# One small matmul moved ahead of a product: the MLP norm's mean between the first products of two blocks

## The chip, the cores and the metric

The kernel runs on one core of a Trainium2 chip. The time is the device time of one execution in microseconds (us). One further execution was recorded by the hardware profiler; its time line (the trace) and its summary page are what the profile is here.

## The reference

The kernel computes a small decoder trunk in float32 for 512 tokens of width 1024. Two layers follow one another, the first with a multi-head latent attention mixer (MLA), the second with gated linear attention (GLA); each has a squared-ReLU MLP with 4096 hidden columns:

```python
def rms_norm(x, gain):
    y = xf * lax.rsqrt(jnp.mean(xf * xf, axis=-1, keepdims=True) + EPS)
    return (y * gain).astype(x.dtype)
def sq_relu_mlp(xn, w_up, w_down):
    hid = jnp.square(jax.nn.relu(xn @ w_up))
    return hid @ w_down
...
        x = x + mix.astype(x.dtype)
        x = x + sq_relu_mlp(rms_norm(x, norm_mlp[i]), mlp_w_up[i], mlp_w_down[i]).astype(x.dtype)
    return rms_norm(x, final_norm)
```

## The kernel before

**Layout.** The residual stream is held transposed, as 8 tiles `xT[j]` of 128 features by 512 tokens. A float32 matrix is cut into a rounded part and a remainder (`split`: ScalarE writes the high part, line 112, VectorE the low part, line 115), and a product is taken as high times high, high times low and low times high. In the MLP these matmuls have 256 columns and are issued by line 826 (`matmuls`): 24 for each product, 16 with the high part of the weights (`wh`) and 8 with the low part (`wl`). "Product" below means such a run of 24.

**The MLP.** The up projection goes through blocks of 512 hidden columns, `up_block(b)` for b = 0 to 7. A block is a list of steps s0 to s7, which form its result with seven products in place of eight (a Strassen scheme: the names 11, 21, 22, T1 to T4 are quadrants of the normalised input and their combinations, prepared by class `QuadNorm`). The down projection is split in the same way (`down_block`, whose left operand is the tile `h`, 48 matmuls to a product). `mlp` pops the steps of the blocks from lists in an order written out by hand.

**The norm.** The gain is applied to the operands at once, the root of the mean only where a product is finished (`finish`, lines 887 to 891, which multiplies by `rstd`). `square` sums the squares of the 8 tiles in `acc` (line 238, VectorE); `mean` (line 255) multiplies `acc` by a matrix of 1/1024, which leaves the mean in a PSUM bank; `Norm.finish` and `rsqrt` (lines 211 to 221) turn it into `rstd` with two ScalarE and three VectorE operations. The float32 matmul of the mean appears as two records in the trace.

**Start of the MLP.** The last output projection of the mixer adds into `xT[7]`, and its square is the last that goes into `acc`. Meanwhile two matmuls whose result is not used (line 1163) and the first product of block 0 run (`s1`: operand tiles x0 to x3, weights `wh` and `wl`). The first product of block 1 has its weights in a tile named `w`, which takes the place that the combination T3 gets afterwards (`s0`, line 907). `combine` and `combined` then form T3 on VectorE and ScalarE.

**Order.** A planner orders the instructions of each engine by their place in the program and by its own estimate of when their inputs are there. `keep_in_program_order` (`kept`) pins an instruction behind the one written before it on the same engine; the first matmul of every product is pinned so (line 839), and so is the mean. On TensorE the order around the change is thus fixed by the text.

**Places in memory.** The pools hold a few spacers (`PADS`, `pad`). The tile `h1` is made 40 elements (160 bytes) longer than needed, and `operand` uses it from element 0 for the first product of a down block that takes this tile, and from element 40 for the others:

```python
                h = dp.tile([P, 8 * TH + 40], F32R, tag="h1", name=uname("h"))
                c = 0 if turn[1] != s else 40
```

Of the kernel before, what the change touches and what calls it, by code (L numbers as in the profile page):

```python
# [49 lines left out]
def trunk_kernel(ctx: ExitStack, tc: tile.TileContext, t_in: dict, out: bass.AP, out_row: bass.AP):  # L50
# [22 lines left out]
    def uname(s):  # L73
        count[0] += 1
        return f"{s}_{count[0]}"
# [69 lines left out]
    def piece(raw, a, n, order=lambda i: i):  # L145
        hi = sb.tile([P, a, n], F32R, tag="wh", bufs=3, name=uname("wh"))
        lo = sb.tile([P, a, n], F32R, tag="wl", bufs=3, name=uname("wl"))
        cut_at.append(split(raw, hi, lo, order=order))
        return hi, lo
# [183 lines left out]
    nrm = Norm(ND, inv_d, "mix", 0, "A")  # L333
# [475 lines left out]
    def mlp(layer, nrm, nxt, final=False):  # L809
# [337 lines left out]
        blocks = [up_block(b) for b in range(NB)]  # L1147
# [18 lines left out]
        for b, t in enumerate(halves(wide_raw())):  # L1166
            fills[b](t)
        kept = tc.keep_in_program_order
        for b in range(2):
            blocks[b].pop(0)()  # L1170
        t = nrm.combine(KH - 1, dp.tile([P, 4, TH], F32, tag="q", bufs=6, name=uname("q")))
        kept(nrm.mean())
        made[1]["21"] = piece(made[1]["a12"], KH, 256)
        kept(cut_at[-1])
        kept(nrm.combined(KH - 1, t))
# [466 lines left out]
    n_mix1 = Mixer(ND, inv_d, "mix", ND, "A")  # L1642
    n_mlp0 = mlp_norm(0)
    mlp0 = mlp(0, n_mlp0, n_mix1)
    out_proj(t_in["mla_w_o"][0], O, n_mlp0, mlp0, begun)
    next(mlp0, None)
# [5 lines left out]
    class Final:  # L1652
# [39 lines left out]
        def row(self, t, c, p):  # L1692
# [19 lines left out]
            for eng, q, cs in ((ACT, ACT, slice(0, 384)), (DVE, SP, slice(384, D))):  # L1712
# [4 lines left out]
                q.dma_start(o[:, cs], y[:, cs])  # L1717

    mlp1 = mlp(1, n_mlp1, Final(), True)
    out_proj(t_in["gla_w_o"][0], Y, n_mlp1, mlp1)  # L1720
    next(mlp1, None)
# [53 lines left out]
```

## Time and profile before

| what | value |
|---|---|
| runs | 1065.54, 1066.1, 1068.97 us; median 1066.1 us |
| the profiled execution's own time | 1065.53 us |
| its span, first to last instruction | 1063.8 us |
| TensorE matmul busy (PE) | 1055.4 us, 99% |
| weight loads (PEld) | 975.8 us, 92% |
| VectorE (DVE) | 856.6 us, 81% |
| ScalarE (ACT) | 642.4 us, 60% |
| mean granted TensorE clock | 0.998 |

Rows of the trace's time line give the start in us from the span's start, the duration in us, the engine, the line, the operation, the tile written and the tiles read, the shape, and how many like instructions are merged (x2). Buffer numbers are left out of names; for a matmul, the moving operand stands first and the weights second (`ps<-x0h,w`). PEld rows are weight loads; a load runs ahead of the matmul that uses it. Matmuls overlap in the pipeline, so a row's duration is longer than the distance to the next row's start; the pace of the array is the distance between starts.

### The profile page before, as it was taken

How to read it: one execution, taken by the hardware profiler on the slowest of the kernel's cores; microseconds unless marked ns; L12 is line 12 of the kernel's file. 1: busy time of each engine (PE TensorE's matmuls, PEld its weight loads, DVE VectorE, ACT ScalarE, POOL GpSimd, SP SyncE). 2: the span in 40 equal slices, each digit the busy share in tenths (PEclk: the TensorE clock that was granted, in tenths of full speed). 3: DMA queues.
4: the chain of work that ended last, by engine and by line, in shares of the span. 5: the costliest groups of instructions: out<-in, count | busy, mean ns of one | idle time of the engine just before them, and what ended most of it. 6: DMA issues, size and time to landing. Idle time of an engine off the chain costs nothing.

```text
span 1063.8 us, 17962 instructions
## 1 busy us (share of the span) xinstructions
PE 1055.4 (99%) x7332; PEld 975.8 (92%) x7332; DVE 856.6 (81%) x1186; ACT 642.4 (60%) x937; POOL 78.8 (7%) x104
## 2 busy tenths in 40 slices
PE   9999999999999999999999999999999999999997
PEld 7788988999999999988788888888999999999986
DVE  6789879899799789967565654678999799799965
ACT  6577645575667777644334734655665667776734
POOL 7400001000000000030000000001000000000000
PEclk9999999999999999999999999999999999999999
DMA  7312017765553663360222211238665555654412
GB/s 219 91 50 80 7 34 217 165 193 145 173 141 118 179 155 112 99 203 26 53 77 80 80 59 61 80 99 218 179 141 154 158 126 159 173 127 117 139 40 79
DMA packets 114946, 127.81 MB, mean 120 GB/s; under 512 B 8640, under 2 KB 86736, under 8 KB 114864
## 3 DMA queue, kind: packets, MB, share of 16 engines
q1 hardware_dynamic: 98832, 108.15, 32.0%
q0 software_dynamic: 13792, 16.80, 10.2%
q10 hardware_dynamic: 2240, 1.73, 0.5%
q8 instruction: 57, 0.93, 0.4%
q14 instruction: 25, 0.20, 0.1%
HBM read 124.56 MB, written 2.10 MB: 119 GB/s over the span
## 4 chain that ended last, share of the span: by engine, by line
PE 96%; DVE 2%; ACT 0%; DMA 0%; issue 0%; ACTq 0%; DVEq 0%
PE ps L826 51%; PE ps L120 13%; PE ps L122 13%; PE ps L121 13%; PE ps L1426 2%; PE ps L137 1%; PE ps L1465 0%; PE ps L1432 0%; PE ps L1412 0%; PE ps L685 0%; PE ps L686 0%; PE ps L684 0%; PE ps L682 0%; PE ps L683 0%; DVE stat L695 0%; DMA gains<-in_gains_dram 0%
## 5 line engine op out<-in xcount | busy, mean ns | idle before, releaser
L112 ACT ACTIVATE wh<-raw 128x1024 fp32r<-128x1024 f32 x208 | 219.8, 1060 | 152.7 <-PE ps L826 99.4
L115 DVE TENSOR_TENSOR wl<-raw,wh 128x1024 fp32r<-128x1024 f32 x208 | 251.8, 1220 | 25.4 <-ACT wh L112 25.1
L826 PE MATMUL ps<-h,wh 128*128 128x256 f32 x1344 | 168.6, 278 | 0.0
L826 PEld LDWEIGHTS ps<-h,wh 128*128 128x128 f32 x1344 | 161.2, 188 | 0.0
L120 PE MATMUL ps<-set,wh 128*128 128x512 f32 x232 | 91.3, 394 | 0.0
L826 PE MATMUL ps<-h,wl 128*128 128x256 f32 x672 | 91.2, 278 | 0.0
L121 PE MATMUL ps<-set,wh 128*128 128x512 f32 x232 | 90.7, 391 | 0.1
L122 PE MATMUL ps<-set,wl 128*128 128x512 f32 x232 | 90.7, 391 | 0.0
L112 ACT ACTIVATE wh<-wraw 128x1024 fp32r<-128x1024 f32 x41 | 43.1, 1057 | 74.2 <-PE ps L122 41.5
L826 PEld LDWEIGHTS ps<-h,wl 128*128 128x128 f32 x672 | 83.6, 188 | 0.0
L879 POOL DMA_DIRECT2D raw<-in_mlp_w_up_dram x20 | 25.8, 1290 | 707.4 <-DMA raw<-in_mlp_w_up_dram 330.5
L891 ACT ACTIVATE q<-q 128x512 f32<-128x512 f32 x64 | 40.3, 630 | 40.2 <-DVE q L890 39.8
L115 DVE TENSOR_TENSOR h<-q,h 128x1024 fp32r<-128x1024 f32 x44 | 53.7, 1222 | 9.1 <-ACT h L112 9.0
L120 PE MATMUL ps<-wh,set 128*128 128x512 f32 x144 | 59.7, 414 | 0.0
L115 DVE TENSOR_TENSOR wl<-wraw,wh 128x1024 fp32r<-128x1024 f32 x41 | 50.3, 1226 | 11.1 <-ACT wh L112 10.8
L122 PE MATMUL ps<-wh,set 128*128 128x512 f32 x144 | 56.3, 391 | 0.0
L121 PE MATMUL ps<-wl,set 128*128 128x512 f32 x144 | 56.2, 390 | 0.0
L121 PEld LDWEIGHTS ps<-set,wh 128*128 128x128 f32 x232 | 43.6, 188 | 9.9 <-DVE set L246 0.9
L122 PEld LDWEIGHTS ps<-set,wl 128*128 128x128 f32 x232 | 43.6, 188 | 9.4 <-DVE wl L115 0.5
L120 PEld LDWEIGHTS ps<-set,wh 128*128 128x128 f32 x232 | 43.5, 188 | 9.0 <-issue 0.2
L112 ACT ACTIVATE h<-q 128x1024 fp32r<-128x1024 f32 x44 | 46.0, 1049 | 0.2
L121 PE MATMUL ps<-hl,wh 128*128 128x512 f32 x96 | 37.4, 389 | 0.0
(512 smaller groups left out, 2789.4 us busy)
## 6 DMA issues: line engine op xcount, KB each, us to landing
raw<-in_mlp_w_down_dram SPq DMA_DIRECT2D x38, 1024.0 KB, 5.2
raw<-in_mlp_w_up_dram SPq DMA_DIRECT2D x70, 512.0 KB, 5.3
wraw<-in_gla_w_in_dram SPq DMA_DIRECT2D x11, 1024.0 KB, 5.1
raw<-in_mlp_w_up_dram POOLq DMA_DIRECT2D x20, 512.0 KB, 7.4
raw<-in_mlp_w_down_dram POOLq DMA_DIRECT2D x6, 1024.0 KB, 9.3
wraw<-in_mla_w_o_dram SPq DMA_DIRECT2D x8, 512.0 KB, 4.8
wraw<-in_gla_w_o_dram SPq DMA_DIRECT2D x8, 512.0 KB, 4.7
wraw_qn<-in_mla_w_uq_dram SPq DMA_DIRECT2D x6, 256.0 KB, 3.4
```

Source lines behind the costliest of these rows:

```text
L112: raised.append(order(ACT.activation(hi, src, AF.Copy)))
L115: return lo_eng.tensor_tensor(lo, src, f(hi), ALU.subtract)
L120: PE.matmul(psum, wh, xh, start=start, stop=False, **kw)
L121: PE.matmul(psum, wh, xl, start=False, stop=False, **kw)
L122: PE.matmul(psum, wl, xh, start=False, stop=stop, **kw)
L137: PE.transpose(psum, src, ident[: src.shape[0], : src.shape[0]])
L826: return PE.matmul(p[:, m * TH : (m + 1) * TH], w[i][:, k - k0, m * P : (m + 1) * P], x[k][j], start=start, stop=stop, skip_group_check=True,)
L879: POOL.dma_start(t, rows(half, trail), accum_op=ALU.add)
L891: ACT.activation(qs, qs, AF.Square)
L1426: PE.matmul(p[:, t * 64 : (t + 1) * 64].rearrange("p (n c) -> p n c", c=m), k[:, sl], later, start=True, stop=True)
```

## The change

The matmul of the mean is written between the first product of block 0 and that of block 1, where it stood behind both and behind `combine`. Both layers run this code. No instruction is added or taken away, and no transfer is written elsewhere.

```diff
         kept = tc.keep_in_program_order
-        for b in range(2):
-            blocks[b].pop(0)()
+        blocks[0].pop(0)()
+        kept(nrm.mean())
+        blocks[1].pop(0)()
         t = nrm.combine(KH - 1, dp.tile([P, 4, TH], F32, tag="q", bufs=6, name=uname("q")))
-        kept(nrm.mean())
         made[1]["21"] = piece(made[1]["a12"], KH, 256)
         kept(cut_at[-1])
         kept(nrm.combined(KH - 1, t))
         pad(up, PADS["up"])
         nrm.finish()
```

## The prediction

> **What bounds the kernel now.** I read the page's busy times first, then the chain that ended last, then what TensorE waited for.
>
> ```profile
> span 1063.8 us, 17962 instructions
> PE 1055.4 (99%) x7332; PEld 975.8 (92%) x7332; DVE 856.6 (81%) x1186; ACT 642.4 (60%) x937; POOL 78.8 (7%) x104
> ...
> PE 96%; DVE 2%; ACT 0%; DMA 0%; issue 0%; ACTq 0%; DVEq 0%
> ...
> PE ps L1599 <- DVE ones L175: 1.2, 1, 1.2
> PE ps L685 <- ACT set L665: 0.3, 1, 0.3
> ```
>
> TensorE is busy for 99% of the span and makes 96% of the chain; in the view of waits it stops for 1.5 us in all, none of it in the MLPs. So only two things can move the time: a new stop of TensorE, or another pace of its matmuls. An earlier `rstd` alone gives nothing, because no matmul waits for it now.
>
> Next I looked at the pace. The time line of layer 0 gives starts of products of 24 matmuls.
>
> ```profile
> 198.92 0.28 PE L826 MATMUL ps<-x4h,wh 128*128 128x256 f32 x1
> ...
> 238.49 0.40 PE L826 MATMUL ps<-h,wh 128*128 128x256 f32 x2
> ...
> 244.09 0.28 PE L826 MATMUL ps<-T0h,wh 128*128 128x256 f32 x1
> ...
> 326.06 0.40 PE L826 MATMUL ps<-h,wh 128*128 128x256 f32 x2
> ...
> 331.67 0.28 PE L826 MATMUL ps<-x4h,wh 128*128 128x256 f32 x1
> ...
> 334.40 0.28 PE L826 MATMUL ps<-T0h,wh 128*128 128x256 f32 x1
> ...
> 391.52 0.40 PE L826 MATMUL ps<-h,wh 128*128 128x256 f32 x2
> ```
>
> From 198.92 to 238.49 lie 14 products, 336 matmuls: 117.8 ns each. From 334.40 to 391.52 lie 21 products, 504 matmuls: 113.3 ns each. The shape is the same and TensorE idles in neither; yet the second stretch is 4.4 ns a matmul faster. The windows show this in both layers (count over time, some two matmuls too many at the edges), at a full clock:
>
> ```profile
> core 0: us, PE busy (x), PEclk, DMA share, GB/s
> 245.00:325.00 80.00, 80.00 (x681) 1.00 0.60 161
> 334.00:391.00 57.00, 57.00 (x505) 1.00 0.50 142
> 792.00:872.00 80.00, 80.00 (x682) 1.00 0.60 162
> 881.00:938.00 57.00, 57.00 (x506) 1.00 0.52 145
> ```
>
> A pace is therefore a state that is kept across products. The reader is to see what ends one: at 238.49, 326.06 and 391.52 stand the three products that use `h1` from element 0. The first leaves the slow pace as it was (244.09 to 326.06 are 29 products, 696 matmuls, 117.8 ns), the second is followed by the fast one.
>
> **The change part by part.** The mean itself, before, in both layers:
>
> ```profile
> 191.79 0.69 DVE L238 TENSOR_TENSOR acc<-acc,tmp 128x512 f32<-128x512 f32 x1
> 192.25 0.19 PEld L826 LDWEIGHTS ps<-x0h,w 128*128 128x128 f32 x1
> 192.36 0.28 PE L826 MATMUL ps<-x0h,w 128*128 128x256 f32 x1
> ...
> 195.00 0.40 PE L826 MATMUL ps<-x3h,w 128*128 128x256 f32 x2
> 195.24 1.02 PE L255 MATMUL ps<-acc,inv 128*128 128x512 f32 x2
> ...
> 196.21 0.28 PE L826 MATMUL ps<-x4l,wh 128*128 128x256 f32 x1
> ...
> 738.83 0.69 DVE L238 TENSOR_TENSOR acc<-acc,tmp 128x512 f32<-128x512 f32 x1
> 739.28 0.19 PEld L826 LDWEIGHTS ps<-x0h,w 128*128 128x128 f32 x1
> ...
> 92.91 0.61 DVE PTl L731
> 93.52 0.04 issue
> 93.56 0.49 PE ps L120
> ```
>
> *Moved work.* The mean occupies TensorE from 195.24 to 196.21, less one matmul of 0.12: 0.85 us. It costs that wherever it stands, so 0.
>
> *New wait.* The last addition into `acc` ends at 191.79 + 0.69 = 192.48. The chain shows 0.04 to 0.05 us from a VectorE end (93.52) to a TensorE start (93.56), so the mean's weight load can start at 192.53. TensorE would be there at 192.25, where `w` is loaded now: 0.28 us of stop. In layer 1, 739.52 + 0.05 against 739.28: 0.29 us. Together +0.57 us, on the path, as all of TensorE is. Behind the waiting instruction are queued all later matmuls; ScalarE and VectorE wait for them only later than now. Before the change this wait was covered by block 1's first product.
>
> *Later on TensorE.* Block 1's first product ends 0.85 + 0.28 = 1.13 us later, hence also the last reads of `w`, whose place T3 takes:
>
> ```profile
> 194.64 1.06 ACT L112 ACTIVATE T3h<-q 128x1024 fp32r<-128x1024 f32 x1 [1.50 <-DVE q L301]
> ...
> 199.74 1.22 DVE L115 TENSOR_TENSOR wl<-raw,wh 128x1024 fp32r<-128x1024 f32 x1
> ...
> 203.16 0.28 PE L826 MATMUL ps<-T3h,wh 128*128 128x256 f32 x1
> ...
> 203.63 0.40 PE L826 MATMUL ps<-T0h,wl 128*128 128x256 f32 x2
> ```
>
> T3h moves from 194.64 to about 195.7 and is used at 203.16: hidden, with over 6 us to spare. If the planner leaves the mean's two ScalarE operations behind it, `rstd` and the `wl` piece of 199.74 come some 1 us later, done at 202.0 and wanted at 203.63: hidden. If it puts them ahead, where ScalarE now idles 1.50 us before T3h, `rstd` is earlier, for which nothing waits. Should the later order leave VectorE behind for some products, its cost is bounded by that 1 us a layer, 2 us; I take 0. No transfer is issued by a moved step, so the queues of SP and POOL keep their order; the mean's PSUM bank is one of three, and a later product that takes it finds it free sooner.
>
> *Pace.* This is the large term, and the trace does not show the new sequence; its bounds are 0 or worse on one side and the fast pace from the start on the other. Now block 1's first product runs at 120.0 ns (192.36 to 195.00: 22 matmuls in 2.64 us), then comes the mean, then 117.8. With the change nothing stands between the product with `w` and the next one. The durations of single weight loads tell where in its beat a state stands:
>
> ```profile
> L826 PEld LDWEIGHTS ps<-x2h,wl 128*128 128x128 f32 x2 | 0.3, 188 | 0.0
> ...
> L826 PEld LDWEIGHTS ps<-x1l,w 128*128 128x128 f32 x2 | 0.4, 192 | 0.0
> L826 PEld LDWEIGHTS ps<-x3h,w 128*128 128x128 f32 x2 | 0.3, 192 | 0.0
> ...
> L826 PEld LDWEIGHTS ps<-T3h,wl 128*128 128x128 f32 x1 | 0.2, 192 | 0.0
> L826 PEld LDWEIGHTS ps<-T0h,wh 128*128 128x128 f32 x1 | 0.2, 188 | 0.0
> ...
> L826 PEld LDWEIGHTS ps<-T0h,wh 128*128 128x128 f32 x1 | 0.2, 192 | 0.0
> L826 PEld LDWEIGHTS ps<-x7h,wl 128*128 128x128 f32 x1 | 0.2, 187 | 0.0
> ```
>
> At the fast pace every load takes 188 ns (first row, at 191.8). With `w` every load takes 192 (next two). At 117.8 every third does; 24 is a multiple of three, so each product starts on the same beat. Before the `h1` product that left the slow pace alone, products began with a load of 188 (the pair at 235.55); before the one that led to the fast pace, with one of 192 (the pair at 323.12). With the change the first load of block 0's next product runs during the last matmul with `w`, where all loads take 192. So I expect the slow pace, but on the second beat, and the `h1` product at 238.49 to do what that at 326.06 does now. The fast pace then starts at 244.09 instead of 331.67: up to 326.06 stand the 29 products counted above, 696 matmuls, 4.4 ns less each, 3.1 us; the `h1` product at 326.06 itself is left as it is. Layer 1 has the same windows: 6.2 us for both.
>
> Sum against the profiled execution: 1065.53 + 0.57 - 6.2 = 1059.9. That execution lies 0.57 under the median 1066.1; on the median it is 1060.5, which I predict.
>
> **The rivals.**
>
> *Fast from the start* (B).
>
> ```profile
> 189.39 0.40 PE L1163 MATMUL ps<-x0h 128*128 128x256 f32 x2
> ```
>
> The `w` product leads straight into the fast pace, as the two unused matmuls of line 1163 do before the fast product at 189.62; both read weights that lie 96 bytes past a multiple of 128, like `w` (the built program puts `w` at byte 214,624 of a partition, x0h at 151,136, `wh` at 34,720, which is 32 past). Another 15 products (195.69 to 238.49 without the `h1` one), 360 matmuls, 1.6 us a layer: 1060.5 - 3.2 = 1057.3. Against it: two matmuls are not 24, and before them ran products of another shape.
>
> *No change of pace* (C). The mean, or the wait before it, was not what set the beat; 117.8 goes on to 331.67 and only the wait counts: 1066.1 + 0.57 = 1066.7; if a single layer changes its beat, 1063.6. For it: the pace after 195.69 follows the same weights and operands as it would then. Against it: the beat is shown to differ with what ran before (238.49 and 326.06).
>
> The Trainium skill, page "TensorE: Matmul & The Clock Gate", section "Back-to-back issue gap", gives the spacing of matmuls by their column count, isolated N / 2.4 + 2.5, which I estimate at 109 ns for 256 columns, and lets weight loads share in it, but no history. By that rule case C holds; the traces show 113.3, 117.8 and 120.0 ns for one shape, so they do not agree with it.
>
> *Slow for longer* (D), on the other side. The beat falls so that neither `h1` product, at 238.49 or 326.06, frees the pace, and the one at 391.52 does. Then 22 products from 331.67 on, 528 matmuls, lose 4.4 ns: 2.3 us a layer, 1066.7 + 4.7 = 1071.4. It decides if the first load of the products after 199 stands on the third beat, which no `h1` product has met in this trace.
>
> **How the numbers follow.** Chances: the forecast 0.43, B 0.19, C 0.25, D 0.13. What this measurement can tell from no change is about 0.3%, 3.2 us: the forecast and B are faster, 0.62; C is the same, 0.25; D slower, 0.13. The range leaves out D and reaches from B less 0.8 us to C with 0.8 us of late VectorE: 1056.5 to 1067.5. The forecast's own range is 1059.9 to 1062.5, from no wait at all to the 2 us of late VectorE.
>
> **What would show it.** The mean's row should follow x3h,wl at once, with a stop of 0.28 us before it and `acc` as what it waited for. `w` should keep 192 ns and 120.0. The windows decide the rest: 245 to 325 should hold some 706 matmuls instead of 681, and products before 238 should begin with a load of 192. If those loads are 188 and the window still holds 681, C is right; if the window from 199 to 238 is fast already, B. The prediction is wrong above all if the beat after `w` is set by something that the loads' durations do not show.

## The result and the profile after

| | median, us | lowest to highest |
|---|---|---|
| before | 1065.88 | 1065.40 to 1068.97 |
| after | 1060.49 | 1060.21 to 1062.29 |

The ratio is 0.9948, 95% interval 0.9935 to 0.9961. The forecast was 1060.5 us. The number came out; two of the steps on the way to it did not. The profiled execution took 1060.21 us, its span is 1058.5 against 1063.8 before. From the page of the changed kernel (the one instruction less is a semaphore event; the matmuls, loads and operations are as many as before):

```profile
span 1058.5 us, 17961 instructions
...
PE 1049.1 (99%) x7332; PEld 969.1 (92%) x7332; DVE 855.6 (81%) x1186; ACT 639.4 (60%) x937; POOL 78.6 (7%) x104
...
PE 98%; DMA 1%; DVE 1%; ACT 0%; issue 0%; ACTq 0%; DVEq 0%
```

TensorE is busy 6.3 us less and the span is 5.3 us shorter, so about 1 us of new standing must be there. The view of waits (TensorE's line, what it waited for, us in all, times, longest) names it:

```profile
PE ps L1599 <- DVE ones L175: 1.2, 1, 1.2
PE ps L826 <- ACT ps L926: 0.9, 2, 0.5
PE ps L685 <- ACT set L665: 0.3, 1, 0.3
```

Twice, once a layer, a product waited for line 926, the ScalarE copy that seeds an accumulator. That was not forecast. Around the change itself, in the time line:

```profile
191.86 0.68 DVE L238 TENSOR_TENSOR acc<-acc,tmp 128x512 f32<-128x512 f32 x1
192.60 0.30 PEld L255 LDWEIGHTS ps<-acc,inv 128*128 128x128 f32 x2 [0.21 <-DVE acc L238]
193.14 0.19 PEld L826 LDWEIGHTS ps<-x0h,w 128*128 128x128 f32 x1 [0.24 <-issue]
195.72 1.06 ACT L112 ACTIVATE T3h<-q 128x1024 fp32r<-128x1024 f32 x1 [2.51 <-DVE wl L115]
199.88 1.22 DVE L115 TENSOR_TENSOR wl<-raw,wh 128x1024 fp32r<-128x1024 f32 x1
201.02 0.68 DVE L221 SCALAR_TENSOR_TENSOR rstd<-mt,mt 128x512 f32<-128x512 f32 x1
```

Starts of products in layer 0, to be held against those of before (198.92, 238.49, 244.09, 326.06, 331.67):

```profile
199.26 0.28 PE L826 MATMUL ps<-x4h,wh 128*128 128x256 f32 x1
...
222.51 0.39 PE L826 MATMUL ps<-T0h,wh 128*128 128x256 f32 x1 [0.48 <-ACT ps L926]
...
238.96 0.28 PE L826 MATMUL ps<-h,wh 128*128 128x256 f32 x1
...
244.56 0.28 PE L826 MATMUL ps<-T0h,wh 128*128 128x256 f32 x1
...
323.46 0.28 PE L826 MATMUL ps<-h,wh 128*128 128x256 f32 x1
...
329.06 0.28 PE L826 MATMUL ps<-x4h,wh 128*128 128x256 f32 x1
```

After stands 0.34 us behind before at 199, 0.47 behind at 239 and at 244, and 2.61 ahead at 329. So the gain is made between 244 and 323, as forecast. But between 199 and 239 a loss and a gain have nearly cancelled. The windows (us, TensorE busy, count of matmuls, clock) show where; first before, then after:

```profile
224.00:238.00 14.00, 14.00 (x121) 1.00 0.51 120
771.00:782.00 11.00, 11.00 (x96) 1.00 0.41 75
```

```profile
199.00:221.00 22.00, 22.00 (x189) 1.00 0.49 140
224.00:238.00 14.00, 14.00 (x126) 1.00 0.63 167
245.00:325.00 80.00, 80.00 (x708) 1.00 0.61 163
771.00:782.00 11.00, 11.00 (x99) 1.00 0.62 146
792.00:872.00 80.00, 80.00 (x708) 1.00 0.58 156
```

245 to 325 holds 708 matmuls, where 706 were forecast and 681 stood before. But 224 to 238 is fast already (126 for 121): the slow pace ended at 222, not at 244. It ended at the new stop. Its making, in the rows of before, then of after:

```profile
218.91 0.69 DVE L890 SCALAR_TENSOR_TENSOR q<-ps,rstd 128x512 f32<-128x512 f32 x1 [1.17 <-PE ps L826]
...
220.17 0.58 ACT L926 ACTIVATE ps<-mt 128x512 f32<-128x512 f32 x1
...
221.53 0.28 PE L826 MATMUL ps<-T0h,wh 128*128 128x256 f32 x1
```

```profile
219.48 1.23 DVE L115 TENSOR_TENSOR wl<-raw,wh 128x1024 fp32r<-128x1024 f32 x1 [0.72 <-ACT wh L112]
220.62 0.68 DVE L890 SCALAR_TENSOR_TENSOR q<-ps,rstd 128x512 f32<-128x512 f32 x1
...
221.34 0.63 ACT L891 ACTIVATE q<-q 128x512 f32<-128x512 f32 x1 [0.94 <-DVE q L890]
221.88 0.58 ACT L926 ACTIVATE ps<-mt 128x512 f32<-128x512 f32 x1
```

Block 0's last `finish` (line 890) reads an accumulator; only then can line 926 seed it for block 1. Before, VectorE was idle when the product ended and finished at once. After, the planner has put a `wl` piece ahead of it, and that piece waited for its `wh`. The seed came at 222.46 instead of 220.75 and TensorE stood: from 221.53 to 222.51 the lag grows from 0.34 to 0.98, 0.64 us, and 0.60 us in layer 1. That is more than the 0.9 us of the view of waits, which counts from the end of the last matmul's row, and rows reach beyond the next start.

### The profile page after: what moved, and what is told of

The parts are those of the page before. It is cut to its first block, busy times and chain, and to the rows that moved or that the text cites. A ratio compares the mean times of both kernels' runs of the same rounds, so it can differ in the third digit from the quotient of the medians.

```text
span 1058.5 us, 17961 instructions
## 1 busy us (share of the span) xinstructions
PE 1049.1 (99%) x7332; PEld 969.1 (92%) x7332; DVE 855.6 (81%) x1186; ACT 639.4 (60%) x937; POOL 78.6 (7%) x104
## 4 chain that ended last, share of the span: by engine, by line
PE 98%; DMA 1%; DVE 1%; ACT 0%; issue 0%; ACTq 0%; DVEq 0%
PE ps L826 51%; PE ps L120 13%; PE ps L122 13%; PE ps L121 13%; PE ps L137 2%; PE ps L1426 2%; DMA xT<-in_x_dram 1%; PE ps L1465 0%; PE ps L685 0%; PE ps L686 0%; PE ps L684 0%; PE ps L683 0%; PE ps L682 0%; PE ps L1432 0%; PE ps L1412 0%; PE ps L255 0%
## 5 line engine op out<-in xcount | busy, mean ns | idle before, releaser
L112 ACT ACTIVATE wh<-raw 128x1024 fp32r<-128x1024 f32 x208 | 218.8, 1057 | 122.2 <-PE ps L826 64.1
```

The lines of the kernel that those rows point to most:

```text
L112: raised.append(order(ACT.activation(hi, src, AF.Copy)))
```

## The experiments

Below, the fast pace is 113.3 ns a matmul and the slow one 117.8; on the first beat of the slow pace a product begins with a load of 188 ns, on the second with one of 192. The edits are shown shortened. Theory H is the forecast: second beat behind `w`, released by the `h1` product at 238. Theory R holds that a stop of TensorE alone releases the slow pace, so that the move of the mean worked only through its side effect.

### 1. The seed on time

```diff
 finish:  v["fin"] = DVE.scalar_tensor_tensor(qs, ...)
 s6:      with tc.high_priority() if b == 1 else nullcontext(): seed(v["p1"])
          with tc.issue_after(made[0]["fin"].ins) if b == 1 else nullcontext(): product(v["b2"], v["s"], "T2", False)
```

> The changed kernel with one thing mended: the copy that seeds block 1's second accumulator (line 926) is put ahead of the Square beside it, and the remainder wl for that product (line 115) is pinned behind the finish of block 0 (line 890), so that the seed should be there before 221.9 us and TensorE should not stop there. TensorE's order is untouched. Theory H (the forecast: second beat from the w product on, released by the h1 product at 238): products go on at 117.8 ns until 239 and at 113.3 ns from 244 on. A layer saves the stop of 0.63 us and loses 6 products x 24 x 4.44 ns = 0.64 us, so the time stays that of the changed kernel, 1060.5 us. Theory R (only the stop at 222 released the pace): 117.8 ns up to 326 or longer, 35 products, 840 matmuls x 4.44 ns = 3.7 us a layer less 0.63 us: 1060.5 + 6.2 = 1066.7 us, or more where the h1 product at 326 does not release it either.

Measured 1060.64 us (1060.39 to 1061.47), 0.9949 of before. The wait for line 926 is gone. Windows, and the first load of the product ahead of the `h1` product:

```profile
224.00:238.00 14.00, 14.00 (x121) 1.00 0.62 168
245.00:325.00 80.00, 80.00 (x707) 1.00 0.61 163
771.00:782.00 11.00, 11.00 (x96) 1.00 0.58 144
```

```profile
L826 PEld LDWEIGHTS ps<-T0h,wh 128*128 128x128 f32 x1 | 0.2, 192 | 0.0
```

Slow up to the `h1` product, on the second beat, fast behind it, in both layers: H, to the number. The stop in the changed kernel bought the fast pace 6 products earlier and cost about what that was worth (0.6 us for 0.5 a layer, by the lags above).

### 2. Only the stop, in the old place

```diff
 seed:  for _ in range(2 if b == 1 else 1): ACT.activation(v["b2"], src, AF.Copy)
```

> The kernel before, mean in its old place, with one more copy of the seed of block 1 (line 926 twice). The second copy comes behind a ScalarE piece of 1.04 us, so the seed is there at about 222.2 us in place of 220.75 and TensorE should stop for some 0.7 us at 221.5, and likewise near 771 in layer 1. Theory R (a stop of TensorE is enough to release the slow pace): 113.3 ns from 222 on; 35 products up to the h1 product at 326, 840 matmuls x 4.44 ns = 3.7 us less the stop of 0.7: 3.0 us a layer, 1066.0 - 6.0 = 1060.0 us, without any move of the mean. Theory H alone (only the h1 products on the right beat release it): the stop is only lost, 1066.0 + 1.4 = 1067.4 us, with 117.8 ns up to 326.

Measured 1061.51 us (1060.88 to 1065.40), 0.9963 (0.9950 to 0.9977). The profiled execution, 1064.59 us, is one of the two long ones: when the first MLP began it was already 3.2 us behind the kernel before, all of it lost in the kernel's first 15 us (waits at lines 120 and 121), which the edit does not touch. Its wait, two windows, and the first load of the product at 239.7:

```profile
PE ps L826 <- ACT ps L926: 1.2, 2, 0.6
```

```profile
245.00:325.00 80.00, 80.00 (x707) 1.00 0.60 159
771.00:782.00 11.00, 11.00 (x96) 1.00 0.20 33
```

```profile
L826 PEld LDWEIGHTS ps<-T0h,wh 128*128 128x128 f32 x1 | 0.2, 192 | 0.0
```

Neither theory: the stop left the pace slow (96 matmuls from 771 to 782), but moved it from the first beat, 188, to the second, 192, and the next `h1` product released it. By the starts of products a stop cost 0.75 us and the product behind it another 0.11, 1.7 us in both layers: 1065.9 + 1.7 - 6.2 = 1061.4.

### 3. A pair of unused matmuls behind the mean

```diff
+        kept(nrm.mean()); pair(mp.tile([P, 4 * TH], F32, tag="d", bufs=2, name=uname("ps")))
 # pair(t): the two matmuls of line 1163, x0h by x0h, into t
```

> The kernel before, mean in its old place, with two more unused matmuls of the form of line 1163 (x0h by x0h, their weights 96 bytes past a multiple of 128) right behind the mean; VectorE's order is the same, one ScalarE pair changes places. Cost 2 x 0.12 us a layer, 0.5 in all. Theory H (after a matmul whose load takes 192 ns the products start on the second beat, and the h1 product at 238 then releases the slow pace): first loads of the products after 199 take 192 ns in place of 188, 117.8 ns up to 239, 113.3 ns from 244 on, 29 products x 24 x 4.44 ns = 3.1 us a layer: 1066.0 + 0.5 - 6.2 = 1060.3 us. Theory B (the pair itself starts the fast pace, as at the head of the MLP): fast from 196 on, 4.7 us a layer: 1066.0 + 0.5 - 9.4 = 1057.1 us. Theory R (only a stop releases): 1066.5 us, slow up to 326.

Measured 1057.49 us (1056.94 to 1058.25), 0.9919 (0.9907 to 0.9932), less than either kernel of the comparison.

```profile
199.00:221.00 22.00, 22.00 (x197) 1.00 0.58 164
771.00:782.00 11.00, 11.00 (x96) 1.00 0.75 186
```

The pair started the fast pace at once, in both layers (197 matmuls instead of 189): theory B. The profiled execution took 1058.25 us. In its layer 1 TensorE, now earlier, lost 0.13 us at 758.6 for a load that was not ready, and was slow from there to the `h1` product at 781 (96): 8 products, some 1.0 us with the stop. Whether that also makes the 0.4 us by which the median lies above the expected 1057.1 is not shown.

### 4. No `h1` product at element 0, in the changed kernel

```diff
-                    c = 0 if turn[1] != s else 40
+                    c = 40
```

> The changed kernel with the tile h1 always used from element 40, so that no product has the operand at element 0 that the forecast took as the release. Theory R (the stop at 222 released the pace and the state keeps itself): still slow 196 to 222 and 113.3 ns from 222 on; the three down products that ran at 116.7 ns run at 113.3 ns, 3 x 48 x 3.4 ns = 0.5 us a layer: 1060.5 - 1.0 = 1059.5 us. Theory H (the h1 products are needed to hold or to set the fast pace): 117.8 ns again somewhere behind 239; up to the end of the layer's MLP some 80 products x 24 x 4.44 ns = 8.5 us a layer, up to 1077 us.

Twelve runs, median 1068.85 us, fall into three groups: 1059.1 to 1060.9 us (3 runs), 1068.4 to 1069.7 (6), 1077.8 to 1078.5 (3), with a granted clock of 0.998 or 0.999 in all. The profile is of the first group and fast from 222 on in both layers (R):

```profile
245.00:325.00 80.00, 80.00 (x708) 1.00 0.60 162
792.00:872.00 80.00, 80.00 (x708) 1.00 0.56 154
```

A layer that stays slow to its end costs some 9 us (experiment 5), so by their times the groups are: both layers released by the stop, one, none. By that reading 12 of 24 layers were released; a trace shows only the first group. A stop is thus a toss, and the `h1` products are what hides a lost toss in the changed kernel: there it costs 6 products, 0.6 us, in place of 9 us.

### 5. Neither the stop nor the `h1` product

Edits 1 and 4 together.

> The changed kernel with the seed on time (no stop at 222) and the tile h1 always used from element 40. Theory H (what released the slow pace at 239 to 244 in the run with the seed on time was the h1 product from element 0): nothing releases it now, 117.8 ns from 196 to the end of the MLP in both layers. The slowest runs of the changed kernel with h1 at 40 took 1077.8 to 1078.5 us; less their two stops of 0.63 us: 1076.8 us, and every run alike. Rival (something else near 239 releases it, such as the first down product): 1060.6 less 1.0 for the h1 products: 1059.6 us.

Measured 1076.55 us (1076.52 to 1076.91).

```profile
245.00:325.00 80.00, 80.00 (x681) 1.00 0.61 164
334.00:391.00 57.00, 57.00 (x487) 1.00 0.52 148
792.00:872.00 80.00, 80.00 (x682) 1.00 0.58 154
```

117.8 ns to the end of both MLPs in the profile, and the four runs lie within 0.4 us. The `h1` product at element 0 is what released the pace in experiment 1.

### 6. The pair, without the `h1` products

Edits 3 and 4 together, on the kernel before.

> The kernel before with the unused pair behind the mean, and the tile h1 always used from element 40. If the fast pace that the pair starts keeps itself: 113.3 ns in all products behind 196, the three products a layer at 116.7 ns gone, 3 x 48 x 3.4 ns = 0.5 us a layer: 1057.5 - 1.0 = 1056.5 us, all runs within 2 us. Rival (the fast pace is lost now and then, and the h1 products bring it back): single runs longer by up to 9 us, as with the changed kernel and h1 at 40.

The rival: 1055.94 to 1056.90 us in 3 runs, 1065.05 to 1066.55 in 9 (median 1065.36).

```profile
245.00:325.00 80.00, 80.00 (x709) 1.00 0.59 160
792.00:872.00 80.00, 80.00 (x681) 1.00 0.53 146
```

In this profile, of a long run, layer 0 is fast throughout; layer 1 lost the pace at 760.6, where a load came 0.10 us late, and nothing brought it back. A stop of 0.13 us at 757.7 had left it fast; the like stop in front of the same product ended the fast pace in experiment 3. That is the toss seen in traces.

### 7. `w` 64 bytes further on, in the changed kernel

```diff
-w = ... up.tile([P, KH, 256], F32R, tag=f"T{KH - 1}{x}", ...)
+w = ... up.tile([P, KH * 256 + 32], F32R, tag=f"T{KH - 1}{x}", ...)[:, 16 : 16 + KH * 256].rearrange(...)
```

The built program then has `w` 32 bytes past a multiple of 128 (214,432); other tiles move by multiples of 128.

> The changed kernel with the tile w placed 64 bytes further on, so that it lies 32 bytes past a multiple of 128 like wh; order of all engines unchanged. Theory W (the address of w is what ends the fast pace of block 0's first product): w's product at 113.3 ns and fast from there; 24 x 6.4 ns + 9 products x 24 x 4.44 ns = 1.1 us a layer: 1060.5 - 2.2 = 1058.3 us, up to 1060.5 if TensorE, being earlier, only waits longer for the seed at 222. Theory M (the mean, with the wait for acc, ends the fast pace): 117.8 ns in w's product and behind it; 1060.4 us where the next h1 product or the stop releases it, up to 1066 where only that at 326 does.

Loads in `w`'s product (first of eight like rows), and waits:

```profile
L826 PEld LDWEIGHTS ps<-x1h,w 128*128 128x128 f32 x4 | 0.7, 188 | 0.0
```

```profile
PE ps L826 <- ACT ps L926: 1.8, 2, 1.0
```

On the pace theory W holds: 188 ns and 113.3 in `w`'s product, and fast behind it, in both layers. On the time it fails: 1062.44 us (1061.24 to 1062.68), slower than the changed kernel. TensorE arrived earlier and only waited longer for the same seed (1.8 us for 0.9), and it stopped twice more, 0.25 us at 207.4 and 0.20 us at 752.6, for a `wh` piece (line 112); both stops left the pace fast. In layer 0 a load that came 0.08 us late had ended the fast pace at 218.8 already; the stop at 222 left it slow, up to the `h1` product at 240, which cost 0.6 us against the changed kernel.

### 8. The pair behind `w`'s product, in the changed kernel

```diff
-        blocks[1].pop(0)()
+        blocks[1].pop(0)(); pair(mp.tile([P, 4 * TH], F32, tag="d", bufs=2, name=uname("ps")))
```

> The changed kernel with two more unused matmuls of the form of line 1163 right behind block 1's first product, the one with w. Theory P (two such matmuls start the fast pace wherever they stand): fast from 196.7 on, 9 products x 24 x 4.44 ns = 1.0 us a layer less 0.24: 1060.5 - 1.5 = 1059.0 us, up to 1060.5 if the wait for the seed grows. Theory Q (they work only behind a short stop of TensorE such as that behind the mean; behind w's product they are two more loads of 192 ns): 117.8 ns from 196.7, second beat, then as the changed kernel: 1061.0 us.

Measured 1060.30 us (1060.16 to 1061.61).

```profile
199.00:221.00 22.00, 22.00 (x189) 1.00 0.50 142
224.00:238.00 14.00, 14.00 (x126) 1.00 0.57 152
```

Slow up to 221 (189 matmuls): theory Q. The stop at 222 then released it, as in the profile of the changed kernel. Two such matmuls start the fast pace behind the mean and not behind the 24 of `w`.

### 9 to 12. Towards a kernel without the slow stretch

**9.** Edit 7 on the kernel before:

> The kernel before, mean in its old place, with only the tile w placed 64 bytes further on; order of all engines unchanged. Theory W (the address of w ends the fast pace, the mean does not): 113.3 ns in w's product and in the 44 products behind it up to the h1 product at 326 that are slow now: 24 x 6.7 ns + 44 x 24 x 4.44 ns = 4.85 us a layer: 1065.9 - 9.7 = 1056.2 us; where TensorE, being earlier, comes to stop for VectorE (near 222 or 759) and falls into the slow pace until the next h1 product, up to 1.4 us a layer more: 1056.2 to 1059. Theory M (behind the mean in its old place the pace is slow whatever stood before): only 24 x 6.7 ns a layer are saved, 1065.6 us, or 1060 if the beat changes and the h1 product at 238 releases it.

Measured 1058.88 us (1058.59 to 1059.67). In the profile `w`'s product is fast, but behind the mean 117.8 came in both layers, on the second beat (192), released by the `h1` product at 238 in layer 0; in layer 1 it turned fast at 750.7, inside a product and without a stop that the trace shows:

```profile
199.00:221.00 22.00, 22.00 (x189) 1.00 0.57 173
746.00:766.00 20.00, 20.00 (x176) 1.00 0.58 185
```

The time lies in theory W's range, but not for W's reason: in layer 0 it is the last case of theory M. So `w`'s address ends the fast pace, and the mean can do so as well.

**10.** Edit 9, and in block 0 `third` leaves its `finish` to `s7`, behind the addition of line 976:

```diff
 third:  if b: finish(c, 0, second)
 s7:     i = DVE.tensor_tensor(c, pairs(v["b2"]), pairs(v["p5"]), ALU.add)
         with nullcontext() if b else tc.issue_after(i.ins):
             [finish(q[1][:, 2 * h : 2 * h + 2], h, second) for h in ((1,) if b else (0, 1))]
```

> As the one before (w 64 bytes on, mean in its old place), and in block 0 the finish of the third product's half (line 890) put behind the addition of line 976, which frees the accumulator that the next product waits for: VectorE frees it 0.6 us earlier. If the stops near 222 and 759 come from this addition, TensorE does not stop there and no layer falls back into the slow pace: 1056.2 us, runs alike. If they come from elsewhere: as the one before.

Measured 1059.41 us (1059.31 to 1060.98): nothing gained. There was no stop at 759, but in layer 0 the slow stretch of 196 to 239 was the larger loss, as in 9; layer 1 turned fast at 749.4, behind a load 0.02 us late.

**11.** Edits 1 and 7 together, mean between the products:

> The changed kernel (mean between the first products) with w 64 bytes further on and the seed of block 1 on time. The pace is the fast one in both this and the kernel before with w 64 bytes on, so the difference of the two is what the move itself costs: the wait for acc, 0.28 + 0.29 us forecast, plus what TensorE waits for the later pieces (0.3 us at 207 in the run with w 64 bytes on): 1056.2 + 0.6 + up to 0.6 = 1056.8 to 1057.4 us; if a stop throws a layer back into the slow pace, up to 1.2 us more.

Measured 1059.93 us (1059.77 to 1061.53), outside what was expected: behind the mean the pace was slow in both layers (189 matmuls from 199 to 221), where in 7, with the same mean in the same place, it was fast. Since the paces differ, this run says nothing of the cost of the move alone.

**12.** All three edits on the kernel before (pair behind the mean, `w` 64 bytes on, later `finish`):

> The kernel before, mean in its old place, with three edits that the runs so far point to: the unused pair behind the mean, w 64 bytes further on, and in block 0 the finish of the third product's half behind the addition of line 976. If the mean deals the pace anew and the pair behind it makes it the fast one: 113.3 ns in w's product and in all products from 196 to the h1 product at 238, in both layers. Against the run with the pair alone (1057.5 us) it saves 2 x 24 x 6.7 ns = 0.3 us, and in layer 1 the stop near 758 with the slow pace behind it, 0.5 to 1.1 us: 1056.1 to 1056.7 us. If a stop for VectorE or ScalarE comes elsewhere, since TensorE is still earlier, and the pace falls back until 238: 1057.5 us or more.

```profile
199.00:221.00 22.00, 22.00 (x196) 1.00 0.61 166
746.00:766.00 20.00, 20.00 (x172) 1.00 0.57 180
```

Measured 1057.70 us (1057.28 to 1060.69), 0.9917 (0.9904 to 0.9930): the case of the last sentence. The profile is of a long run, 1059.97 us. Layer 0 is fast from the pair on; layer 1 lost the pace at 748.8, where a load came 0.07 us late. It is not to be told from experiment 3, which stays the simplest of the best.

## Why the prediction was right, and where it was not

*The bound.* Right: outside the MLPs TensorE's rows kept their distances to 0.1 us. The first MLP began 0.07 us late and ended 2.61 ahead, the second gained 2.7 more, which makes the span's 5.3 us.

*Moved work, new wait.* Right. `acc` ended at 192.54, the mean's load began at 192.60, and without the wait TensorE would have been there at 192.32 (192.25, and the MLP began 0.07 later): 0.28 us, the forecast's figure. By 199 the lag had grown by 0.27 in layer 0 (0.34 less the 0.07) and in layer 1.

*T3h, `rstd`, late VectorE.* T3h started at 195.72, forecast 195.7, and was hidden. `rstd` was finished 1.9 us later than before (201.70 for 199.82), not "some 1 us", since a `wl` piece went ahead of its last step. The term taken as 0 is the mis-sized one: the later order left the seed of block 1 late and cost 0.64 and 0.60 us, 1.24 in all, within the 2 us given as its bound. It was not the piece that follows the mean that came late, but one 20 us behind it, whose slack before had been 0.7 us (seed there at 220.75, wanted at 221.42).

*`w`'s pace and the beat.* Right, in both layers: `w`'s loads took 192 ns and its matmuls 120.0 from the eighth on (the first seven loads, behind the mean, took 187 to 190; before, the first two took 188), and the products behind them began with a load of 192. The rows at 196.3, 199.1 and 746.3 of the changed kernel:

```profile
L826 PEld LDWEIGHTS ps<-x4h,wh 128*128 128x128 f32 x1 | 0.2, 192 | 0.0
```

```profile
L826 PEld LDWEIGHTS ps<-T0h,wh 128*128 128x128 f32 x1 | 0.2, 192 | 0.0
```

That the load beside the last `w` matmul sets the beat is not shown: in experiments 9 and 11 products began with 192 behind the mean alone.

*The release.* This step failed in the profiled execution: the `h1` product at 239 found the fast pace, which the unforeseen stop had released at 222.5. As a mechanism it holds: experiment 1 shows the step as written, experiment 5 that the pace stays slow without it. In the profiles of all these kernels, every slow stretch that reached an `h1` product from element 0 with products beginning with 192 ended there (13 of them), and those beginning with 188 (the first of each layer before) did not.

*The sum.* Forecast 0.57 - 6.2 = -5.6. The profile has 0.54 of waits, 1.24 of stops, and in each layer a gain of 0.5 between the stop and the `h1` product and of 3.1 behind it: -7.2; together -5.4. The time agrees because the stop, which was missed, released the pace early enough to pay for most of itself. That the two nearly cancelled is luck; experiment 1, with neither, takes the same time. A stop that does not release would add 0.6 us a layer, which the runs after, 1060.2 to 1062.3, do not resolve.

*The rivals.* B failed: behind `w` at its old address the pace was slow in all ten layers profiled with the mean ahead of it; there `w`'s product is what ends the fast pace (7), and two matmuls of its kind start it only elsewhere (3, 8). C failed by 708 matmuls for 681; with it fails, for these operands, a spacing that follows from column count and weight load alone, as the Trainium skill gives it (page "TensorE: Matmul & The Clock Gate", section "Back-to-back issue gap"): one shape ran at 113.3, 116.7, 117.8 and 120.0 ns. D, a beat that no `h1` product releases, was met in no kernel with `h1` at element 0; what a slow pace costs that nothing releases is 1076.5 us (experiment 5).

## What to carry to other kernels

Where one engine is busy throughout, read its pace by stage, not its busy share: here 4 ns a matmul, kept for 80 us, was worth more than any wait. A moved instruction shifts a planner's order far behind it, so look for the piece with the least slack in the next 30 us, and do not book "late" at zero because the first pieces are hidden. A single profile does not show a toss: run the kernel with the safety net taken away, and the spread of the runs shows it.

## What the runs showed of the hardware

For 128x256 matmuls at a granted clock of 1.00 the pace depended on where operands lie. By byte address in the built program modulo 128 (moving operand, weights) it was 120.0 ns at 96 and 96; 116.7 at 64 and 32 (`h1` at element 0); at 96 and 32 either 113.3 or 117.8, whichever state had been entered. Moving `w` by 64 bytes took its product from 120.0 to 113.3 ns where the pace around it was fast.

What dealt the state anew was the mean or a stop of TensorE, even a short one: 0.07 us ended the fast pace in 12, while 0.08 us at 759.4 in 9 left it. Which state came of it was not the same each time (the like stop in 3 and 6; by the run times 12 of 24 in experiment 4; behind the mean ahead of `w`, fast in 7 and slow in 11). What decides it stays open, as does why it turned fast without a stop in 9. A pair of matmuls at 96 and 96 behind the mean, or behind the last output projection at the head of the MLP, was followed by the fast pace in each layer profiled.

In the kernels with `w` 64 bytes on, every product with T operands at the fast pace, 44 to 55 of 196, took 14 ns longer (2.73 us for 2.72); it takes back 0.6 to 0.8 us of what they won. The time lies in the matmuls with T3l and in the one that follows them: 117.9 ns for T3l against 113.5 in the changed kernel. T3l has the place of `w`'s low part, and in these builds it alone of the T and x tiles lies 224 bytes past a multiple of 256, the others 96. That this address is the cause is not shown by a run of its own.
